# Last convolution in the gating tile, mixed blocks loaded a K tile at a time, conditioning sums by VectorE, attention's place kept free of the last weights

## The chip, the cores and the metric

The kernel runs on one core of a Trainium2 chip. A core has five engines that work through instruction lists of their own and meet at semaphores: TensorE (PE, with its weight loads as PEld), VectorE (DVE), ScalarE (ACT), GpSimd (POOL) and SyncE (SP), which here only issues loads. Transfers run on 16 DMA engines. The metric is the device time of one execution in microseconds (us), as a median over runs; a shorter time is better.

## The reference

One layer of a hybrid backbone over 2048 tokens of width 1024 (a grid of 32 rows by 64 columns), with 256 context tokens. Everything is float32.

```python
mod_l = jnp.split((jax.nn.silu(c) @ ada_w[l] + ada_b[l])[:, None, :], 6, axis=-1)
h = _modulate(_rmsnorm(x, norm1_g[l]), mod_l[0], mod_l[1])
z = h @ w_in[l]            # columns: q, k, v (512 each), gating u, v (256 each), conv a, gate (256 each)
kvc = hc @ w_in[l][:, ATT_W:3 * ATT_W]                       # keys, values of the context
att = _neighbourhood_attention(q, k, v, kc, vc, na_rpb[l], rows)   # 8 x 16 window, 8 heads
sg = _spatial_gating(u, v, ...)      # gelu(u) * (chunks of 128 tokens of norm(gelu(v)), mixed by w_s)
cv = _conformer_conv(a, gate, ...)   # 31-tap depthwise convolution, group norm, silu
y = jnp.concatenate([att, sg, cv], axis=-1) @ w_out
x = x + mod_l[2] * y
h2 = _modulate(_rmsnorm(x, norm2_g[l]), mod_l[3], mod_l[4])
x = x + mod_l[5] * _conv_ffn(h2, ffn_w_up[l], ffn_conv_w[l], ffn_conv_b[l], ffn_w_down[l])
return _rmsnorm(x, final_norm_g)
```

## The kernel before

The 2048 tokens are four blocks of 512 (`TB`), numbered 0 to 3. A float32 product is made of three matmuls on a high and a low part of each operand (suffixes `h` and `l`); the parts come from a copy on ACT (L228, L249) and a subtraction on DVE or POOL (L229, L252). All matmuls go through `mm` (L204), all loads through `load` (L195, queue of SP), most stores through `store` (L198, queue of POOL).

The program has these stages, by the profile's time. A setup to about 60 us makes block 0's input. **Stage 1**, to about 300 us, weaves several generators together: `stage1()` with the projections of blocks 0 and 1 (k, convolution, gating, v, q), the row statistics of the input (`stats`), `ada_rest` and the convolution of block 0 (`conv_range(0)`). **Attention**, to about 1010 us, is `attend()`: 128 units, each a band of rows, a pair of heads, a column block and one head of the pair. A unit has `scores` (matmuls into the bank `s`, one reduction on DVE that adds the bias and finds the maximum, L695, the exponential on ACT, L698), `turned` (transposes `tp`, copied to `pt` by ACT, L728, and DVE, L730) and, for each two units, `values`. Between these the generator `fill()` puts the projections of blocks 2 and 3 and the output projections, and from units 0, 45 and 80 on the convolutions of blocks 1, 2 and 3 run beside them, one step for each unit. After that come the end of the output projection, the feed-forward layer's upper half (to about 1925 us) and its lower half.

PE's instructions up to the end of attention are pinned to the order of the program. A scheduler orders the other engines by priority and by its own estimate of times: what is inside `hot` gets a high priority, `issue_after` forbids an instruction to stand ahead of another.

Names that the change touches:

- PSUM in stage 1: a ring `g` of five banks for the projections, one bank `m`, two banks `ad`. `m` takes the mean and scale banks of a convolution (`cvm`, `cvv`, `cvr`), the row norms' factors (`h1ms` to `h3ms`, made by `rstd`) and the gating's mixing (`sgp`, made by `gating_tail` and emptied by the DVE instruction `sgm`, L509).
- `conv_range(b)`: two accumulators `cv` (two channel tiles), begun by ACT (L569) and continued by 30 taps each on DVE (L575); then mean (L585), variance, scale (L610), silu (L613), split, and a store into `mixd`. The accumulators come from a ring `acc` of two, so each convolution waits until the one before has been stored.
- The gating tile (tag `gu`, one buffer): u and v of one block; it is free once the block's gating has been stored in `mixd`.
- `ada_rest`: the conditioning columns that are not needed at once. For each of 16 groups two 512 KB tiles `adaf` are loaded (a ring of three), scaled by silu(c) row by row on ACT (L965, eight instructions), and added up on POOL (L968, L969, L970: 1024, 512 and 256 elements).
- `mixd` holds the concatenated [att, sg, cv] of each block in memory; `load_mix(b)` brings all eight K tiles, high and low part (`mxh`, `mxl`), into the place of the blocks' h, for the output projection.
- Weights come through `load_w`: a staging tile, and rings of three for the high and the low part; every fourth weight takes a buffer of another pool, in the list `wxp`, as long as that list is not empty. The attention pool is opened over the place of that pool and of the stage's other ones.
- `h2xa`, `h3xa`: pieces of the input of blocks 2 and 3; `qq`, `kk`, `vt`, `vcx`, `bias_t`: what a unit of attention loads; `qs`, `ks`, `vs` are where q, k, v lie in memory.

Of the kernel before, what the change touches and what calls it, by code (L numbers as in the profile page):

```python
# [143 lines left out]
def tile_hybrid_block(ctx: ExitStack, tc: tile.TileContext, a, out):  # L144
# [157 lines left out]
    mbufs = 1  # L302

    def add_square(acc, x, n, name, eng, pool):
        if acc is None:
# [258 lines left out]
    def conv_range(b):  # L564

        hb = hcv[b]
        acc = [jp.tile([P, TB], F32, bufs=2, tag="acc", name=f"cv{b}{ct}") for ct in range(2)]
# [34 lines left out]
        nc.vector.reciprocal(col, col)  # L602
        yield
# [47 lines left out]
    qk, biases = {}, {}  # L651

    def scores(band, pr, cb, j, pool):

        if (band, pr, j) not in qk:
            head_tiles(band, pr, j, pool)
        qq, kk = qk[band, pr, j]
        r0, nr = ROWS[band]
        kr0, knr, kc0, knc = key_box(band, cb)
        n = knr * knc  # L660
        nch, rp = chunking(band, cb)
        ck = rp * knc
        rt, ct = RTYPE[band], CTYPE[cb]
        nm = f"{band}{pr}{cb}{j}"
        if (band, pr, ct, j) not in biases:
            bt = bias_tile(pool)
            load(bt[:, 512 - n:512], a[f"bias{rt}{ct}"][2 * pr + j])
            biases[band, pr, ct, j] = bt
        bt = biases[band, pr, ct, j]
        if cb == 0 and j == 0:  # L670
            heads[band, pr] = pair_tiles(band, pr, pool)
        vcx, hl, rs = heads[band, pr]
        if j == 0:
            vt = pool.tile([P, 4, P], F32, tag="vt", name=f"vt{band}{pr}{cb}", bufs=4)
            vsr = vs[0:SEQ].rearrange("(r c) f -> r c f", c=64)
            for i in range(nch):
                load(vt[0:ck, i, :],
                     vsr[kr0 + i * rp:kr0 + (i + 1) * rp, kc0:kc0 + knc, pr * P:(pr + 1) * P])
            steps[band, pr, cb] = vt, [], []
        if cb == 3 and (band, pr) != (NB - 1, 3):  # L680
            head_tiles(band + (pr == 3), (pr + 1) % 4, j, pool)
        s = pp.tile([P, 1024], F32, tag="s", name="s" + nm)
        qs_ = slice(cb * P, (cb + 1) * P)
        kv = kk[:, 0:1024].rearrange("p (r c) -> p r c", c=64)[
            :, kr0 - r0:kr0 - r0 + knr, kc0:kc0 + knc]
        so = s[:, 512 - n:512].rearrange("p (r c) -> p r c", c=knc)
        for i in range(2):
            mm(so, qq[:, i, qs_], kv, start=(i == 0), stop=(i == 1))
        for i in range(2):
            mm(s[:, 512:768], qq[:, i, qs_], kk[:, 1024:], start=(i == 0), stop=(i == 1))  # L690
        sb = pool.tile([P, 768], F32, tag="sb", name="sb" + nm, bufs=3)
        mx = cp.tile([P, 1], F32, tag="mx", name="mx" + nm, bufs=3)
        w = slice(512 - n, 768)

        x = nc.vector.tensor_tensor_reduce(out=sb[:, w], in0=s[:, w], in1=bt[:, w], scale=-1.0,  # L695
                                           scalar=3.0e38, op0=ALU.add, op1=ALU.min, accum_out=mx)
        dve_marks.append(x.ins)
        nc.scalar.activation(sb[:, w], sb[:, w], AF.Exp, bias=mx, scale=-1.0, accum_out=rs[:, cb, j:j + 1])  # L698
        steps[band, pr, cb][1].append(sb)
# [76 lines left out]
    def attend(pool, fill, sides):  # L776
# [62 lines left out]
    def load_mix(b, ks_):  # L839
# [3 lines left out]
        more_mix(b, ks_)  # L843

# [87 lines left out]
    jp = wpool_.__enter__()  # L932
# [21 lines left out]
    def ada_rest():  # L954


        for g0 in range(8, 24, 4):
            res = adpool.tile([P, 4, 256], F32, tag="adar", bufs=1, name=f"adar{g0}")
            for i in range(4):
# [8 lines left out]
                nc.gpsimd.tensor_tensor(t, t, t_, op=ALU.add)  # L968
                nc.gpsimd.tensor_tensor(t[:, 0:2, :], t[:, 0:2, :], t[:, 2:4, :], op=ALU.add)  # L969
                nc.gpsimd.tensor_tensor(res[:, i, :], t[:, 0, :], t[:, 1, :], op=ALU.add)  # L970
# [40 lines left out]
    def stage1():  # L1011
# [22 lines left out]
        rstd("h3", TB)  # L1034
        yield from proj_q((1,))
# [14 lines left out]
    def fill():  # L1050
# [602 lines left out]
```

## Time and profile before

| | |
|---|---|
| time of three runs | 2357.55, 2360.74, 2363.66 us; median 2360.74 |
| the profiled execution's own time | 2365.48 us |
| its span | 2363.7 us |
| PE busy | 2268.4 us, 96% of the span |
| DVE, ACT, POOL busy | 72%, 48%, 34% |
| mean granted clock of TensorE | 0.982 |
| HBM traffic | 471 MB, 199 GB/s over the span |

The profile is one execution, recorded by the hardware, and all durations below are its. A row of waits reads "engine tile line <- what released it: total us, times, longest us". A row of the timeline reads "start, duration, engine, line, operation, out<-in", with the idle time of the engine ahead of it and its releaser in brackets. A row of groups has the count, then the busy time and the mean in ns, then the idle time ahead. The granted clock is a share of full speed.

### The profile page before, as it was taken

The numbers are of one execution on the slowest core, as the hardware profiler recorded it, in microseconds if no ns is written. First come the engines' busy times: TensorE is split into PE (matmuls) and PEld (weight loads), VectorE is DVE, ScalarE is ACT, GpSimd is POOL, SyncE is SP. The second block draws the span as 40 slices with busy tenths as digits, with TensorE's granted clock in tenths as the row PEclk, the third lists the DMA queues.
The fourth block names the chain that finished last, engine by engine and source line by source line (L and its number), as shares of the span: only waits on it lengthen the run. The fifth ranks groups of instructions, "written<-read, shape, count | busy, mean of one in ns | idle before, by whom it ended". The sixth has DMA issues, their size and how long they took to land.

```text
span 2363.7 us, 34634 instructions
## 1 busy us (share of the span) xinstructions
PE 2268.4 (96%) x12474; PEld 1898.5 (80%) x12474; DVE 1710.7 (72%) x2552; ACT 1138.6 (48%) x2019; POOL 793.8 (34%) x844
## 2 busy tenths in 40 slices
PE   7999999999899899999999999999999999999998
PEld 5889777997788688878787788778788878888886
DVE  4787556556685694697888887788888777578565
ACT  4765643347455446564444443434333445454443
POOL 0255412111011132225566665455656432002000
PEclk8999999999999999999999999999999999999999
DMA  9675486557879679662444533745553368557653
GB/s 347 230 263 172 168 263 188 180 168 231 258 199 285 199 211 289 231 204 85 138 170 146 181 134 108 270 179 211 210 208 111 98 232 298 196 191 249 204 194 116
DMA packets 203868, 473.63 MB, mean 200 GB/s; under 512 B 21808, under 2 KB 70832, under 8 KB 202672
## 3 DMA queue, kind: packets, MB, share of 16 engines
q1 hardware_dynamic: 166160, 359.20, 47.5%
q0 software_dynamic: 31488, 105.93, 12.0%
q10 hardware_dynamic: 6048, 6.29, 0.8%
q8 instruction: 98, 1.61, 0.3%
q14 instruction: 74, 0.61, 0.1%
HBM read 352.06 MB, written 119.28 MB: 199 GB/s over the span
## 4 chain that ended last, share of the span: by engine, by line
PE 52%; DVE 15%; issue 13%; DMA 12%; ACT 4%; POOL 2%; SPq 1%; POOLq 0%; DVEq 0%; ACTq 0%
PE po L204 4%; PE p L1481 4%; PE pu L1481 4%; PE obank L204 3%; PE pk L204 3%; DMA adaf<-in_ada 3%; PE pv L1481 3%; PE s L204 2%; PE tp L210 2%; PE tp L204 2%; PE pq L204 2%; DMA wds<-in_w_down 2%; SPq L195 1%; DVE cv L575 1%; PE tg L204 1%
## 5 line engine op out<-in xcount | busy, mean ns | idle before, releaser
L575 DVE SCALAR_TENSOR_TENSOR cv<-hconv,cst,cv 128x512 f32<-128x512 f32 x240 | 215.6, 940 | 11.4 <-ACT cv L569 11.2
L1103 DVE TENSOR_TENSOR dw<-wd,dw 128x512 fp32r<-128x512 f32 x154 | 114.1, 749 | 103.3 <-ACT dw L1102 100.8
L1481 PE MATMUL pu<-ah,dw 128*128 128x512 f32 x792 | 181.7, 390 | 0.0
L698 ACT ACTIVATE sb<-sb,mx 128x544 f32<-128x544 f32 (+3 forms) x128 | 106.3, 830 | 154.8 <-DVE mx L695 148.8
L695 DVE CUSTOM_DVE_ANT_0 sb<-s,bias_t 128x544 f32<-128x544 f32 (+3 forms) x128 | 105.1, 821 | 101.7 <-PE s L204 78.3
L1481 PEld LDWEIGHTS pu<-ah,dw 128*128 128x128 f32 x792 | 148.7, 188 | 31.8 <-issue 1.0
L1102 ACT ACTIVATE dw<-wd 128x512 fp32r<-128x512 f32 x154 | 96.0, 628 | 159.7 <-PE pu L1481 58.3
L1481 PE MATMUL p<-ah,dw 128*128 128x512 f32 x528 | 122.5, 394 | 2.4 <-DVE u L1330 2.4
L1481 PE MATMUL pv<-ah,dw 128*128 128x512 f32 x528 | 120.3, 389 | 0.0
L1481 PEld LDWEIGHTS p<-ah,dw 128*128 128x128 f32 x528 | 100.2, 190 | 24.3 <-DVE u L1330 2.9
L204 PE MATMUL s<-kk,qq 128*128 128x256 f32 (+4 forms) x512 | 102.5, 323 | 16.3 <-DVE mx L695 10.2
L204 PEld LDWEIGHTS s<-kk,qq 128*128 128x128 f32 x512 | 89.5, 192 | 34.5 <-DVE mx L695 14.7
L1481 PEld LDWEIGHTS pv<-ah,dw 128*128 128x128 f32 x528 | 99.1, 188 | 20.6
L1367 ACT ACTIVATE c<-c 128x512 f32<-128x512 f32 x88 | 55.3, 630 | 124.9 <-DVE c L1365 124.6
L210 PE MATMUL tp<-cst,sb 128*128 128x128 f32 (+2 forms) x672 | 97.1, 275 | 13.0 <-DVE pt L730 9.0
L210 PEld LDWEIGHTS tp<-cst,sb 128*128 128x128 f32 (+2 forms) x672 | 79.9, 138 | 31.6 <-DVE pt L730 9.9
L1103 POOL TENSOR_TENSOR ah<-ra,ah 128x512 fp32r<-128x512 f32 x22 | 32.9, 1510 | 210.2 <-ACT ah L1102 208.8
L1102 ACT ACTIVATE ah<-ra 128x512 fp32r<-128x512 f32 x154 | 93.9, 617 | 10.6 <-DMA ra<-actd 10.5
L1103 DVE TENSOR_TENSOR ah<-ra,ah 128x512 fp32r<-128x512 f32 x132 | 92.2, 701 | 4.2 <-ACT ah L1102 4.2
L1365 DVE SCALAR_TENSOR_TENSOR cs<-gb,cst,cs 128x512 f32<-128x512 f32 x84 | 62.9, 749 | 21.9 <-ACT cs L1363 21.6
L728 ACT ACTIVATE pt<-tp 128x384 f32<-128x384 f32 (+2 forms) x128 | 61.2, 478 | 36.6 <-PE tp L210 36.0
L965 ACT ACTIVATE adaf<-adaf,silu_c 128x256 f32<-128x256 f32 x128 | 54.2, 497 | 50.5 <-DMA adaf<-in_ada 50.5
(1662 smaller groups left out, 7044.7 us busy)
## 6 DMA issues: line engine op xcount, KB each, us to landing
ra<-actd SPq DMA_DIRECT2D x70, 512.0 KB
wg<-in_w_up SPq DMA_DIRECT2D x44, 512.0 KB
wu<-in_w_up SPq DMA_DIRECT2D x44, 512.0 KB
actd<-tt POOLq DMA_DIRECT2D x88, 256.0 KB, 2.4
wd<-sd SPq DMA_DIRECT2D x40, 512.0 KB
actd<-c POOLq DMA_DIRECT2D x66, 256.0 KB, 2.4
adaf<-in_ada SPq DMA_DIRECT2D x32, 512.0 KB
qq<-qs SPq DMA_DIRECT2D x64, 256.0 KB
```

What stands on the lines that cost most here:

```text
L204: x = nc.tensor.matmul(*args, **kw)
L210: x = nc.tensor.transpose(*args)
L575: nc.vector.scalar_tensor_tensor(acc[ct], hb[:, ct, k:k + TB], cvw[:, ct, k:k + 1], acc[ct], op0=ALU.mult, op1=ALU.add)
L695: x = nc.vector.tensor_tensor_reduce(out=sb[:, w], in0=s[:, w], in1=bt[:, w], scale=-1.0, scalar=3.0e38, op0=ALU.add, op1=ALU.min, accum_o ...
L698: nc.scalar.activation(sb[:, w], sb[:, w], AF.Exp, bias=mx, scale=-1.0, accum_out=rs[:, cb, j:j + 1])
L728: nc.scalar.activation(dst, src, AF.Copy)
L965: nc.scalar.activation(t[:, k, :], t[:, k, :], AF.Copy, scale=silu_c[:, k0 + k, 0:1])
L1102: nc.scalar.activation(hl[:, 0, :], src, AF.Copy)
L1103: eng.tensor_tensor(hl[:, 1, :], src, hl[:, 0, :].bitcast(F32), op=ALU.subtract)
L1365: nc.vector.scalar_tensor_tensor(to, gb[:, i, o + d:o + d + TB], fcw[:, f, d:d + 1], ps, op0=ALU.mult, op1=ALU.add)
L1367: nc.scalar.activation(c, c, AF.Silu)
L1481: nc.tensor.matmul(ps[i], w[:, ww, sl], ah[:, aa, :], start=start and k_ == 0 and m == 0, stop=(k_ == NP - 1 and m == 2), skip_group_check ...
```

## The change

It has six parts. The number of instructions of each kind stays the same, except that 48 additions go from POOL to DVE.

1. The accumulators of the last convolution (b = 3), and one tile of squares of the output projection, are parts of the gating tile after the last gating (`rest`), not of the ring `acc`.
2. `rstd`, and `gating_tail` for blocks 0 and 1, take a bank of the ring `g` instead of `m`.
3. `conv_range` pauses one step more ahead of the rescaling.
4. The loads of the first ten units of attention are placed at normal priority instead of the high one.
5. `mix_steps(b)` places the loads of mixed blocks 0 and 1 one K tile at a time, each behind attention's latest bias or vt load, woven into the convolution and gating projections of block 3 (block 0) and into the output projection (block 1).
6. `ada_rest` adds on DVE, and the list `wxp` is emptied ahead of the q projection of block 1, so that stage 1's last weights take the common rings and attention's place comes free sooner.

```diff
+    def rest_tile():
+        if not rest:
+            rest.append(jp.tile([P, 4 * TB], F32, tag="gu", bufs=1, name="rest"))
+        return rest[0]
...
     def rstd(name, n):
-        ps = pp.tile([P, TB], F32, tag="m", bufs=mbufs, name=name + "ms")
+        ps = g_bank(name + "ms")
...
     def gating_tail(b):
...
-            ps = pp.tile([P, TB], F32, tag="m", bufs=mbufs, name=f"sgp{b}{ct}")
+            ps = g_bank(f"sgp{b}{ct}") if b < 2 else pp.tile([P, TB], F32, tag="m", bufs=mbufs, name=f"sgp{b}{ct}")
...
     def conv_range(b):
-        acc = [jp.tile([P, TB], F32, bufs=2, tag="acc", name=f"cv{b}{ct}") for ct in range(2)]
+        if b == NB - 1:
+            acc = [rest_tile()[:, (1 + ct) * TB:(2 + ct) * TB] for ct in range(2)]
+        else:
+            acc = [jp.tile([P, TB], F32, bufs=2, tag="acc", name=f"cv{b}{ct}") for ct in range(2)]
...
         nc.vector.reciprocal(col, col)
         yield
+        yield
...
-    def scores(band, pr, cb, j, pool):
+    def scores(band, pr, cb, j, pool, loads=None):
+        with (loads or hot)():
             ...   # the loads of qq, kk, bias, vcx, vt; att_load[0] keeps the latest bias or vt load
+        with hot():
             ...   # matmuls, reduction, exponential
...
-                with hot():
-                    scores(*units[u + 2], pool)
+                scores(*units[u + 2], pool, nullcontext if u < 8 else None)
...
+    def mix_steps(b):
+        load_mix(b, ())
+        for k in (4, 5, 6, 7, 0, 1, 2, 3):
+            with tc.issue_after(att_load[0]):
+                more_mix(b, (k,))
+            yield
...
-                nc.gpsimd.tensor_tensor(t, t, t_, op=ALU.add)
-                nc.gpsimd.tensor_tensor(t[:, 0:2, :], t[:, 0:2, :], t[:, 2:4, :], op=ALU.add)
-                nc.gpsimd.tensor_tensor(res[:, i, :], t[:, 0, :], t[:, 1, :], op=ALU.add)
+                nc.vector.tensor_tensor(t, t, t_, op=ALU.add)
+                nc.vector.tensor_tensor(t[:, 0:2, :], t[:, 0:2, :], t[:, 2:4, :], op=ALU.add)
+                nc.vector.tensor_tensor(res[:, i, :], t[:, 0, :], t[:, 1, :], op=ALU.add)
...
         rstd("h3", TB)
+        wxp.clear()
         yield from proj_q((1,))
...
-        yield from proj_conv(3, h["h3"])
-        yield from proj_gating(3, h["h3"])
+        yield from weave(chain(proj_conv(3, h["h3"]), proj_gating(3, h["h3"])), mix_steps(0), 4.0)
         yield from weave(proj_q((3,)), gating_tail(3), 8.0)
-        yield from out_proj((0, 1))
+        yield from weave(out_proj((0, 1)), mix_steps(1), 0.6)
```

Three places show how instructions move. The first is SP's queue at the start of attention: the last pieces of block 2's input (`h2xa`), pieces of block 3's (`h3xa`), weights (`wa21s`, `wk20s`), and the first unit's `qq` and `kk`. Before:

```order
L195 DMA h2xa_2869<-in_xT 128x512
L195 DMA h2xa_2875<-in_xT 128x512
L195 DMA h3xa_3080<-in_xT 128x512
L195 DMA wa21s<-in_w_f 128x1024
L195 DMA h3xa_3086<-in_xT 128x512
L195 DMA h3xa_3092<-in_xT 128x512
L195 DMA wk20s<-in_w_f 128x1024
L195 DMA h3xa_3098<-in_xT 128x512
L195 DMA qq_3162<-qs 64x1024 x2
L195 DMA kk_3165<-ks 128x768
L195 DMA kk_3165<-ks 128x256
```

In the changed kernel the same place reads:

```order
L195 DMA h2xa_2869<-in_xT 128x512
L195 DMA h2xa_2875<-in_xT 128x512
L195 DMA qq_3162<-qs 64x1024 x2
L195 DMA kk_3165<-ks 128x768
L195 DMA kk_3165<-ks 128x256
L195 DMA bias_t_3168<-in_bias 128x288
L195 DMA vcx_3175<-vs 128x2x128
L195 DMA vt_3179<-vs 96x1x128 x3
L195 DMA qq_3208<-qs 64x1024 x2
L195 DMA kk_3211<-ks 128x768
L195 DMA kk_3211<-ks 128x256
L195 DMA bias_t_3170<-in_bias 128x288
```

The first `qq` and `kk` stand right behind the last `h2xa`; the weights and all pieces of `h3xa` come after the first two units' loads of q and k.

The second is SP's queue in the middle of attention, ahead of the bias of a new pair of heads (the row `bias_t_3172` at the end); `mxh` and `mxl` are mixed block 0, `vt` and `vcx` pieces of v, the names ending in s staging tiles of weights. Before:

```order
L195 DMA wt3g_1s<-in_w_tok 128x1024
L195 DMA mxh_7544<-mixd 128x512
L195 DMA mxl_7545<-mixd 128x512
L195 DMA mxh_7544<-mixd 128x512
L195 DMA vt_6189<-vs 128x1x128 x4
L195 DMA vt_6259<-vs 120x1x128 x3
L195 DMA vcx_6374<-vs 128x2x128
L195 DMA mxl_7545<-mixd 128x512
L195 DMA mxh_7544<-mixd 128x512
L195 DMA mxl_7545<-mixd 128x512
L195 DMA wu30s<-in_w_f 128x1024
L195 DMA bias_t_3172<-in_bias 128x360
```

In the changed kernel:

```order
L195 DMA wt3g_1s<-in_w_tok 128x1024
L195 DMA vt_6195<-vs 128x1x128 x4
L195 DMA vt_6267<-vs 120x1x128 x3
L195 DMA vcx_6384<-vs 128x2x128
L195 DMA mxh_6021<-mixd 128x512
L195 DMA mxl_6022<-mixd 128x512
L195 DMA mxh_6021<-mixd 128x512
L195 DMA mxl_6022<-mixd 128x512
L195 DMA wu30s<-in_w_f 128x1024
L195 DMA bias_t_3172<-in_bias 128x360
```

Between the k loads of the pair before and this bias, 14 of the 16 loads of mixed block 0 stood before (two further ahead) and 8 stand now; the other 8 come behind the next two k loads.

The third is ACT in the last third of attention: `sb` are exponentials, `pt` copies of transposes, `att` and `cvsq` splits ahead of stores. Before, the start of the last convolution (`cv_7791<-hconv_5932`) stands among the ends of block 2's (`cv_5997`, `cv_5998`):

```order
L613 ACTIVATE cv_5997<-cv_5997,cst 128x512
L698 ACT_TABLE_LOAD
L698 ACTIVATE sb_7952,rs_7628<-sb_7952,mx_7953 128x616
L228 ACTIVATE cvsq_7835<-cv_5997 128x512
L760 ACTIVATE att_7627<-obank 128x8x32
L728 ACTIVATE pt_7996<-tp_7997 128x384
L569 ACTIVATE cv_7791<-hconv_5932,cst 128x512
L613 ACT_TABLE_LOAD
L613 ACTIVATE cv_5998<-cv_5998,cst 128x512
L698 ACT_TABLE_LOAD
L698 ACTIVATE sb_8037,rs_7628<-sb_8037,mx_8038 128x616
```

In the changed kernel both starts stand at an earlier unit, behind the splits of the last gating (`gu_5933`) and the q projection of block 3:

```order
L746 ACTIVATE pt_7483<-tp_7484 128x384
L716 ACTIVATE sb_7476,rs_7224<-sb_7476,mx_7477 128x768
L249 ACTIVATE wo02h<-wo02s 128x1024
L568 ACTIVATE q_7501<-pq_7426 128x512
L584 ACTIVATE rest<-hconv_5932,cst 128x512
L716 ACTIVATE sb_7524,rs_7224<-sb_7524,mx_7525 128x616
L584 ACTIVATE rest<-hconv_5932,cst 128x512
L778 ACTIVATE att_7223<-obank 128x8x32
L746 ACTIVATE pt_7568<-tp_7569 128x384
L716 ACTIVATE sb_7603,rs_7224<-sb_7603,mx_7604 128x616
```

The two starts moved from the end of block 2's convolution to the unit in which the last gating is stored.

More of the change, by code (lines that the diff above doesn't have):

```diff
@@ L302, in tile_hybrid_block @@
     mbufs = 1
+    jp_ = [None]
+    rest = []
+    def rest_tile():
+        if not rest:
+            rest.append(jp.tile([P, 4 * TB], F32, tag="gu", bufs=1, name="rest"))
+        return rest[0]
     def add_square(acc, x, n, name, eng, pool):
-        if acc is None:
+        if acc is None and pool is jp_[0]:
+            sq = rest_tile()[:, 0:TB]
+        elif acc is None:
             sq = pool.tile([P, 4 * TB], F32, tag="gu", bufs=1, name="sq" + name)[:, 0:TB]
@@ L649, in pair_tiles @@
         return vcx, hl, rs
-    qk, biases = {}, {}
-    def scores(band, pr, cb, j, pool):
[L655 to L699, printed above, removed]
@@ new lines, in tile_hybrid_block @@
+    qk, biases, att_load = {}, {}, [None]
+    def scores(band, pr, cb, j, pool, loads=None):
+        with (loads or hot)():
+            if (band, pr, j) not in qk:
+                head_tiles(band, pr, j, pool)
+            qq, kk = qk[band, pr, j]
+            r0, nr = ROWS[band]
+            kr0, knr, kc0, knc = key_box(band, cb)
+            n = knr * knc
+            nch, rp = chunking(band, cb)
+            ck = rp * knc
+            rt, ct = RTYPE[band], CTYPE[cb]
+            nm = f"{band}{pr}{cb}{j}"
+            if (band, pr, ct, j) not in biases:
+                bt = bias_tile(pool)
+                att_load[0] = load(bt[:, 512 - n:512], a[f"bias{rt}{ct}"][2 * pr + j])
+                biases[band, pr, ct, j] = bt
+            bt = biases[band, pr, ct, j]
+            if cb == 0 and j == 0:
+                heads[band, pr] = pair_tiles(band, pr, pool)
+            vcx, hl, rs = heads[band, pr]
+            if j == 0:
+                vt = pool.tile([P, 4, P], F32, tag="vt", name=f"vt{band}{pr}{cb}", bufs=4)
+                vsr = vs[0:SEQ].rearrange("(r c) f -> r c f", c=64)
+                for i in range(nch):
+                    att_load[0] = load(vt[0:ck, i, :],
+                         vsr[kr0 + i * rp:kr0 + (i + 1) * rp, kc0:kc0 + knc, pr * P:(pr + 1) * P])
+                steps[band, pr, cb] = vt, [], []
+            if cb == 3 and (band, pr) != (NB - 1, 3):
+                head_tiles(band + (pr == 3), (pr + 1) % 4, j, pool)
+        with hot():
+            s = pp.tile([P, 1024], F32, tag="s", name="s" + nm)
+            qs_ = slice(cb * P, (cb + 1) * P)
+            kv = kk[:, 0:1024].rearrange("p (r c) -> p r c", c=64)[
+                :, kr0 - r0:kr0 - r0 + knr, kc0:kc0 + knc]
+            so = s[:, 512 - n:512].rearrange("p (r c) -> p r c", c=knc)
+            for i in range(2):
+                mm(so, qq[:, i, qs_], kv, start=(i == 0), stop=(i == 1))
+            for i in range(2):
+                mm(s[:, 512:768], qq[:, i, qs_], kk[:, 1024:], start=(i == 0), stop=(i == 1))
+            sb = pool.tile([P, 768], F32, tag="sb", name="sb" + nm, bufs=3)
+            mx = cp.tile([P, 1], F32, tag="mx", name="mx" + nm, bufs=3)
+            w = slice(512 - n, 768)
+            x = nc.vector.tensor_tensor_reduce(out=sb[:, w], in0=s[:, w], in1=bt[:, w], scale=-1.0,
+                                               scalar=3.0e38, op0=ALU.add, op1=ALU.min, accum_out=mx)
+            dve_marks.append(x.ins)
+            nc.scalar.activation(sb[:, w], sb[:, w], AF.Exp, bias=mx, scale=-1.0, accum_out=rs[:, cb, j:j + 1])
+            steps[band, pr, cb][1].append(sb)
@@ L792, in attend @@
         for u in range(2):
-            with hot():
-                scores(*units[u], pool)
+            scores(*units[u], pool)
             other(2.0)
@@ L931, in tile_hybrid_block @@
     wpool_ = tc.tile_pool(name="proj", bufs=1, side="right")
-    jp = wpool_.__enter__()
+    jp = jp_[0] = wpool_.__enter__()
     b2 = [jp.tile([P, P], F32, name=f"b2_{i}") for i in range(2)]
```

1 line of the change is left out of this document (removed).

## The prediction

> **What bounds the kernel now.** I read the page's busy table first. PE is busy for nearly the whole span, so a change that adds and removes no PE instruction can only win time in which PE stands still or runs at a reduced clock.
>
> ```profile
> PE 2268.4 (96%) x12474; PEld 1898.5 (80%) x12474; DVE 1710.7 (72%) x2552; ACT 1138.6 (48%) x2019; POOL 793.8 (34%) x844
> ```
>
> The windows view gives the stages (first row: all of stage 1; second: attention) and 30 us stretches in which PE was not full. Columns: length, busy time of PE, weight loads, DVE, ACT, POOL, granted clock, DMA share, GB/s.
>
> ```profile
> 60.00:300.00 240.00, 228.80 (x1462) 200.89 (x1462) 165.71 (x215) 149.57 (x283) 105.91 (x90) 0.99 0.63 210
> 300.00:1010.00 710.00, 679.69 (x5007) 584.45 (x5005) 458.46 (x874) 367.84 (x668) 134.72 (x138) 0.98 0.74 224
> 210.00:240.00 30.00, 26.55 (x204) 25.94 (x204) 9.27 (x10) 13.95 (x35) 14.75 (x8) 0.94 0.53 171
> 240.00:270.00 30.00, 25.89 (x140) 21.26 (x139) 13.64 (x10) 20.24 (x40) 17.00 (x9) 0.94 0.53 176
> 300.00:330.00 30.00, 26.07 (x117) 21.26 (x115) 22.34 (x42) 13.08 (x20) 6.90 (x10) 1.00 0.87 294
> 330.00:360.00 30.00, 26.06 (x120) 21.48 (x120) 13.85 (x25) 15.04 (x24) 4.72 (x2) 0.89 0.72 201
> 630.00:660.00 30.00, 25.27 (x203) 23.90 (x204) 20.98 (x42) 12.49 (x28) 0.57 (x1) 0.83 0.73 212
> 780.00:810.00 30.00, 20.31 (x128) 16.44 (x128) 18.55 (x34) 14.24 (x24) 3.46 (x5) 0.85 0.64 183
> 810.00:840.00 30.00, 29.71 (x231) 25.02 (x230) 29.80 (x50) 13.24 (x29) 8.34 (x7) 0.98 0.82 220
> ```
>
> A stall costs twice here: the wait itself, and the stretch at a reduced clock behind it. I price the second as length times (1 minus clock): 30 x 0.06 = 1.8 us in 210:240 and in 240:270, 30 x 0.11 = 3.3 in 330:360, 30 x 0.17 = 5.1 in 630:660, 30 x 0.15 = 4.5 in 780:810, 30 x 0.02 = 0.6 in 810:840: 17.1 us. This is an upper price, since time that PE waits anyway loses nothing to the clock.
>
> The waits of PE, asked for by stage (60:300, 300:370, 600:650, 700:820), say who released each: total, times, longest; one fence for each stage.
>
> ```profile
> PE h2ms L204 <- DVE cv L585: 4.1, 1, 4.1
> PE tp L204 <- ACT v L420: 3.4, 2, 2.9
> PE sgp L204 <- DVE sgm L509: 2.3, 1, 2.3
> PE sgp L204 <- DVE cv L610: 0.8, 1, 0.8
> ```
>
> ```profile
> PE s L204 <- DMA kk<-ks: 5.6, 1, 5.6
> PE s L204 <- DVE mx L695: 1.8, 1, 1.8
> PE tp L210 <- DVE pt L730: 1.1, 1, 1.1
> ```
>
> ```profile
> PE s L204 <- DVE mx L695: 6.6, 1, 6.6
> ```
>
> ```profile
> PE tp L210 <- DVE pt L730: 6.8, 2, 4.9
> PE tp L210 <- ACT pt L728: 2.9, 1, 2.9
> ```
>
> They sum to 35.4 us. With the clock, at most 52.5 us is to be had in these places; what lies behind attention the change does not touch.
>
> **The change part by part.**
>
> *The m bank in stage 1.* h2ms, h3ms and the gating banks of blocks 0 and 1 leave the one-bank ring "m" and take turns in the five-bank ring "g". The three waits on a DVE instruction that empties that bank (4.1, 2.3, 0.8) have no other cause: h2ms waits for a subtraction of the convolution that it has nothing to do with. They sum to 7.2, with the clock of 240:270 9.0. The g ring lengthens by one tile in use, whose wait would be on an eviction by ACT; the nearest rows are the 3.4 of tp behind ACT's v. The additional yield before the rescale gives the reciprocal one more PE step of cover; it removes nothing that the trace shows as long. I take 7.5, ends 3.5 and 9.
>
> *The conditioning sums on DVE.* 16 groups of three additions (1024, 512, 256 elements) leave POOL for DVE.
>
> ```profile
> L968 POOL TENSOR_TENSOR adaf<-adaf,adaf x16: 2374/2412/3065, 94.9 to 266.0; 128x1024 f32<-128x1024 f32 x16
> L252 DVE TENSOR_TENSOR wtv_0l<-wtv_0s,wtv_0h 128x1024 fp32r<-128x1024 f32 x2 | 2.4, 1219 | 4.5 <-ACT wtv_0h L249 4.5
> L229 DVE TENSOR_TENSOR k<-pk,k 128x512 fp32r<-128x512 f32 x4 | 2.7, 671 | 0.0
> L229 DVE TENSOR_TENSOR k<-pk,k 128x256 fp32r<-128x256 f32 x4 | 1.7, 414 | 0.2 <-ACT k L228 0.2
> L575 DVE SCALAR_TENSOR_TENSOR cv<-hconv,cst,cv 128x512 f32<-128x512 f32 x64 | 68.6, 1126 | 2.1 <-ACT cv L569 2.0
> L575 DVE SCALAR_TENSOR_TENSOR cv<-hconv,cst,cv x64: 715/741/3176, 112.3 to 291.2; 128x512 f32<-128x512 f32 x64
> 177.71 6.49 DVE L575 SCALAR_TENSOR_TENSOR cv<-hconv,cst,cv 128x512 f32<-128x512 f32 x4
> 177.73 2.40 POOL L968 TENSOR_TENSOR adaf<-adaf,adaf 128x1024 f32<-128x1024 f32 x1 [9.76 <-ACT adaf L965]
> POOL adaf L968 <- ACT adaf L965: 89.4, 13, 25.7
> ACT adaf L965 <- DMA adaf<-in_ada: 50.5, 22, 7.4
> ```
>
> By DVE rows of the same lengths a group costs 1.219 + 0.671 + 0.414 = 2.30 us, 36.9 for 16. Against that stands what POOL's additions do to DVE: convolution taps take 741 ns as a median but 1126 as a mean, up to 3176, and the slow ones lie beside an L968 as at 177.71, where four take 6.49 us for some 3.0. 64 x (1126 - 741) = 24.6 us come back on the taps alone, and the same happens to some weight splits. DVE's 165.71 us of 240 therefore stays about the same, with 74 us free. A group gets through about 2.5 us sooner, so its buffers return sooner to the loads; ACT, which stood in front of a late load before it could empty v (rows of 210:240: 3.4 of wait, 1.8 of clock), is helped a little, but the load itself paces that. I take 2 of 5.2; the ends are -4 and 5.2, since DVE now stands where POOL stood and waited 89.4 us for ACT.
>
> *Attention's place and first loads.* In SP's order the first qq and kk now follow the last piece of h2 directly; four loads of h3 and three of weights that stood ahead go behind them.
>
> ```profile
> 308.04 1.78 SPq L195 DMA_DIRECT2D h2xa<-in_xT  x2
> 322.12 1.16 SPq L195 DMA_DIRECT2D qq<-qs  x2
> ```
>
> qq was issued 322.12 - 309.82 = 12.3 us after the last h2 piece, kk right behind it, and PE waited 5.6 us for kk. If the new order lets them go even half of that sooner, the wait is gone; its clock (3.3) goes with it. For that the memory of the weights' second pool must be free, which the cleared list gives: the last four weights no longer sit in it. What is late next is h3's input, behind a dozen more issues of about 1 us, and with it DVE, which does those modulations ahead of score reductions; the 1.8 and 1.1 us of this stage's rows are of that kind and may grow. The last weights also have three buffers for each half where every fourth had a fourth one. Of 5.6 + 1.8 + 1.1 + 3.3 = 11.8 I take 8, ends -2 and 11.8.
>
> *Mixed blocks a K tile at a time.* 14 loads of mixed block 0 stood between the second kk and the bias that the next pair of heads needs; 8 stand there now.
>
> ```profile
> 613.81 8.64 SPq L195 DMA_DIRECT2D vt<-vs  x7
> 625.83 0.85 SPq L195 DMA_DIRECT2D bias_t<-in_bias  x2
> 633.87 0.80 DVE L695 CUSTOM_DVE_ANT_0 sb<-s,bias_t 128x616 f32<-128x616 f32 x1 [9.19 <-DMA bias_t<-in_bias]
> ```
>
> SP is never idle for long in front of this bias: the seven vt pieces alone take 8.64 us to issue, 1.23 each. At that price six loads fewer bring the bias some 7 us forward, and it also finds six 256 KB transfers fewer ahead of it in a window with DMA share 0.73. DVE's 9.19 us shrink to 2 or 3, of which PE, one unit ahead, feels none or one. The displaced eight follow at the next pair, where the same row of loads passes without a stall. 6.6 + 5.1 = 11.7; I take 10, ends 3 and 11.7. For block 1 SP's order does not change: nothing.
>
> *Last convolution in the gating tile.*
>
> ```profile
> 784.68 0.81 ACT L569 ACTIVATE cv<-hconv,cst 128x512 f32<-128x512 f32 x1 [8.79 <-DMA mixd<-cv]
> 799.40 0.81 ACT L569 ACTIVATE cv<-hconv,cst 128x512 f32<-128x512 f32 x1 [3.51 <-DMA mixd<-cv]
> 728.11 0.53 POOL L198 DMA_DIRECT2D mixd<-gu  x1 [2.00 <-DVE gu L229]
> DMA to landing us min/median/max: 6.2/6.8/7.4
> 732.31 0.81 ACT L698 ACTIVATE sb<-sb,mx 128x616 f32<-128x616 f32 x1
> ```
>
> ACT stood 8.79 and 3.51 us until block 2's convolution had been stored, with the evictions of attention queued behind it: that is PE's 6.8 + 2.9 = 9.7 and the clock of 4.5 + 0.6. With its own place this wait is gone. The new one is for the gating tile: its second store, issued at 728.11, lands about 734.3 to 735.5, and the two new activations stand in ACT's order right around the exponential that ran at 732.31. ACT may thus stand 2 to 3 us there; PE has a unit of work in hand, and I charge 2. The 30 taps now start 50 us sooner, two for each unit, in a stretch where DVE had slack, instead of in the stretch where it was 29.80 of 30 busy. 14.8 - 2 leaves 12.8; I take 11.5, ends 4 and 14.8.
>
> *Sum.* 7.5 + 2 + 8 + 10 + 11.5 = 39 us off the profiled execution, whose own time is 2365.48: 2326.5. The median of the three runs shown, 2360.74, is 4.7 lower. I cannot see whether the runs that were faster had shorter stalls of this kind; I let 3 us of the gain go for it, so 36 off the median: 2325.
>
> The Trainium skill (TensorE: Matmul & The Clock Gate, Part 1, "What's actually happening") says that the throttled state is the default and that one busy window of about 3.4 us lifts it, at half rate until then. By that rule each of the five drops would cost about 1.7 us, 8.5 in place of 17.1, and the forecast would be some 6 to 7 us less gain, an estimate of 2331. The rows decide against it: 5.1 us in 630:660 and 4.5 in 780:810 are more than one such window.
>
> **The rivals.**
>
> *Half of it comes back elsewhere.* Each stall removed lets PE run into the next late thing: h3's loads in 330:360, a later bias, the gating store, evictions when DVE's slack is used. For it speaks that DVE in 810:840 has no slack and DMA is at 0.87 in 300:330; against it that most of the waits named have a cause in order, not in rate. Half of 39 gives 2360.7 - 19 = 2342.
>
> *Everything goes.* All 52.5 us: 2308. Against it: the loads of the conditioning weights and the gating store remain.
>
> *Slower: DVE stands in line for ACT's scaled conditioning tiles.* POOL's 89.4 us of waiting would fall on DVE, with weight splits and evictions queued behind. 165.7 + 36.9 - 24.6 + 89.4 = 267 us against a stage of 240: 27 us over on rate alone. With the other 37 us gained the kernel is still faster; it turns slower if more than 44 us of the 89.4 reach PE (half of them), since 37 - 44 = -7. At 50 us the time is 2374. For it: DVE executes in order, and single waits of 25.7 us exist. Against it: those waits are POOL's idle time between groups, and DVE's order is laid with other work between them, so an addition need not be at the head while its tile is still far off.
>
> The Trainium skill (same page, "Architectural detail") calls DVE's queue strictly first in, first out, which is what this rival needs; no run here shows yet how much reaches PE.
>
> *It does not do what it says.* kk, the bias and the taps arrive no sooner because the transfers, not the places in the queue, are late (DMA share 0.73 to 0.87 in those windows); only the m bank's 7.5 remain at most, within a stage that waits for weights anyway: 2354 to 2361.
>
> **How the numbers follow.** About 0.3% (7 us) is what a measurement of this kernel can tell from no change. The forecast case has 0.58, 2325, its own range 2317 to 2334; half back 0.22 (2342); everything 0.07 (2308); no effect 0.07; slower by the DVE queue 0.06. The first three are faster, and half of the fourth: 0.89; same 0.05; slower 0.06. The range 2307 to 2347 takes in the first three cases, 0.87 together, less their tails.
>
> **What the changed profile would show.** If right: among PE's waits no h2ms behind cv, no kk near 326, none above 2 us at 600:650 and 700:820; the clock at 0.95 or more in the stretches that answer to 330, 630 and 780; the first qq right behind h2xa on SP; taps with a mean near 750 ns in stage 1. What would make it wrong: new PE waits behind DVE for weights or evictions between 100 and 300, with DVE waiting for ACT's adaf; a PE wait behind h3's modulation after 340; ACT standing more than 4 us at the gating store.

## The result and the profile after

The changed kernel took 2343.11 us as a median of four runs (2336.43 to 2346.47), the kernel before 2361.61 on the same chip: a ratio of 0.992, 95% interval 0.9894 to 0.9946. On another chip, with more runs, it was 0.9926 (0.9908 to 0.9944). That is 18 us saved: inside the range of 2307 to 2347, half of the 36 that were forecast, and what the rival "half of it comes back elsewhere" had said (2342).

The page of the changed kernel, first its span and the busy table:

```profile
span 2341.3 us, 34626 instructions
...
PE 2262.6 (97%) x12474; PEld 1892.8 (81%) x12474; DVE 1699.1 (73%) x2600; ACT 1137.3 (49%) x2019; POOL 713.9 (30%) x796
```

POOL has lost 80 us of work and DVE, with 48 more instructions, has lost 12. The windows of stage 1 and attention (length, then busy time of PE, weight loads, DVE, ACT, POOL, then clock, DMA share, GB/s):

```profile
60.00:300.00 240.00, 239.61 (x1531) 210.78 (x1530) 172.83 (x285) 155.08 (x293) 25.32 (x48) 1.00 0.67 227
300.00:1010.00 710.00, 682.78 (x5020) 585.28 (x5019) 465.14 (x880) 373.59 (x677) 134.86 (x136) 0.99 0.75 226
```

Stage 1 is full: 239.61 of 240 us at full clock, where it was 228.80 at 0.99. Attention is hardly fuller than before (682.78, then 679.69). PE's waits, for the stretches that answer to those of the prediction (60:300, 300:345, 640:675, 755:820):

```profile
PE b2p L204 <- DVE b L972: 0.4, 1, 0.4
```

```profile
PE s L204 <- DVE mx L713: 7.1, 2, 5.4
PE tp L210 <- ACT pt L746: 0.9, 1, 0.9
PE tp L210 <- DVE pt L748: 0.4, 1, 0.4
```

```profile
PE tp L210 <- DVE pt L748: 4.3, 1, 4.3
```

```profile
PE s L204 <- DVE mx L713: 1.8, 1, 1.8
PE tp L210 <- ACT pt L746: 1.2, 1, 1.2
PE tp L210 <- DVE pt L748: 0.5, 1, 0.5
```

Every wait named in stage 1 is gone. The wait for kk at attention's start has become one for a score reduction, of the same size; the wait for the bias has become one of 4.3 us some 50 us later; of the waits of the last convolution, 9.7 us, 3.5 are left.

PE's order is pinned up to the end of attention, so the same matmul group can be found in each trace, and the difference of its start in the two shows where time was won. The table gives this lead over the profiled execution of the kernel before, in us, for the changed kernel and for those of the experiments. At the end of stage 1, kernels with the same code up to there differ by 4 us (14.8 to 18.5), but they differ as much already at 63 us (-0.6 to 3.2); from there each of them gains 15.3 or 15.4. So the change of the lead from row to row says more than its height. Each column is a single execution: that of the kernel before took 2365.48 us, 4 more than its median, and that of last_conv_in_ring 2346.67, 7 less than its median.

| group (its start in the kernel before) | changed | sums_on_pool | rows_in_m_bank | start_as_before | mix_whole | mix_spread | last_conv_in_ring | no_pause_last_conv | before_sums_on_dve |
|---|---|---|---|---|---|---|---|---|---|
| first matmul with weight wg00 (63.2) | -0.6 | 2.9 | 1.0 | 1.9 | 3.2 | 2.8 | 2.9 | 1.6 | 2.5 |
| last gating bank of stage 1 (292.6) | 14.8 | 5.7 | 12.3 | 17.2 | 18.5 | 18.1 | 18.3 | 16.9 | 14.5 |
| scores of the 1st unit (331.7) | 20.6 | 11.5 | 18.1 | 18.6 | 24.3 | 23.9 | 24.1 | 22.8 | 15.3 |
| 6th unit (357.0) | 13.5 | 4.1 | 10.1 | 15.9 | 16.5 | 16.5 | 16.8 | 16.0 | 12.2 |
| 54th unit (614.7) | 14.5 | 4.7 | 12.1 | 16.3 | 18.7 | 19.4 | 16.9 | 16.8 | 11.0 |
| 58th unit (640.6) | 23.7 | 13.9 | 21.3 | 25.5 | 21.5 | 28.6 | 26.2 | 26.1 | 13.9 |
| 72nd unit (701.8) | 16.7 | 7.0 | 12.4 | 15.3 | 20.5 | 21.7 | 20.6 | 18.3 | 14.7 |
| 89th unit (780.5) | 16.3 | 5.5 | 13.0 | 15.8 | 18.8 | 18.5 | 20.6 | 18.6 | 15.4 |
| 118th unit (911.5) | 25.1 | 16.7 | 21.6 | 23.9 | 30.6 | 30.2 | 20.2 | 26.8 | 14.8 |
| 128th unit (960.7) | 18.9 | 8.6 | 15.7 | 16.7 | 23.0 | 23.4 | 13.5 | 25.0 | 14.8 |
| lower half's first group (1987.4) | 24.1 | 12.0 | 20.2 | 17.4 | 26.0 | 22.3 | 18.6 | 31.7 | 18.4 |

The column of the changed kernel tells where: 15.4 us in stage 1 (-0.6 to 14.8); nothing at attention's start, where 5.8 are won up to the first scores and 7.1 lost behind them (14.8, 20.6, 13.5); 2.2 around the mixed block, where 9.2 are won at the bias and 7.0 lost behind it (14.5, 23.7, 16.7); 8.8 at the last convolution (16.3 to 25.1); and a loss of 6.2 at attention's end that no term of the forecast had (25.1 to 18.9). The last row lies behind 1000 us of code that is the same in all; what is won or lost there (from -1.1 to +6.7) differs from execution to execution.

### The profile page after: what moved, and what is told of

Read it like the earlier page. It is cut to its first block, busy times and chain, and to the rows that moved or that the text cites. A ratio compares the mean times of both kernels' runs of the same rounds, so it can differ in the third digit from the quotient of the medians.

```text
span 2341.3 us, 34626 instructions
## 1 busy us (share of the span) xinstructions
PE 2262.6 (97%) x12474; PEld 1892.8 (81%) x12474; DVE 1699.1 (73%) x2600; ACT 1137.3 (49%) x2019; POOL 713.9 (30%) x796
## 4 chain that ended last, share of the span: by engine, by line
PE 33%; issue 9%; DVE 5%; DMA 3%; ACT 0%; POOL 0%; SPq 0%; POOLq 0%; DVEq 0%; ACTq 0%
PE p L1506 4%; PE pu L1506 4%; PE pv L1506 3%; DMA wds<-in_w_down 2%; PE u_9y L1335 1%; PE g_9y L1335 1%; PE u_8y L1335 1%; PE g_8y L1335 1%; PE u_7y L1335 1%; PE g_7y L1335 1%; PE u_6y L1335 1%; PE g_10y L1335 1%; PE g_5y L1335 1%; PE g_4y L1335 1%; PE u_4y L1335 0%
## 5 line engine op out<-in xcount | busy, mean ns | idle before, releaser
L1506 PEld LDWEIGHTS pu<-ah,dw 128*128 128x128 f32 x792 | 148.7, 188 | 31.7 <-issue 1.0
L590 DVE SCALAR_TENSOR_TENSOR cv<-hconv,cst,cv 128x512 f32<-128x512 f32 x180 | 135.2, 791 | 2.5 <-ACT cv L584 2.4
L1506 PEld LDWEIGHTS pv<-ah,dw 128*128 128x128 f32 x528 | 99.1, 188 | 20.5
L204 PEld LDWEIGHTS s<-kk,qq 128*128 128x128 f32 x512 | 88.8, 191 | 30.8 <-DVE mx L713 17.2
L1127 ACT ACTIVATE ah<-ra 128x512 fp32r<-128x512 f32 x154 | 93.8, 617 | 12.2 <-DMA ra<-actd 10.9
L1390 DVE SCALAR_TENSOR_TENSOR cs<-gb,cst,cs 128x512 f32<-128x512 f32 x84 | 62.9, 749 | 20.5 <-ACT cs L1388 20.2
L198 POOL DMA_DIRECT2D ks<-k x60 | 33.0, 554 | 142.0 <-ACT k L228 117.8
```

The costliest lines, as they stand in the source:

```text
L204: x = nc.tensor.matmul(*args, **kw)
L590: nc.vector.scalar_tensor_tensor(acc[ct], hb[:, ct, k:k + TB], cvw[:, ct, k:k + 1], acc[ct], op0=ALU.mult, op1=ALU.add)
L1127: nc.scalar.activation(hl[:, 0, :], src, AF.Copy)
L1390: nc.vector.scalar_tensor_tensor(to, gb[:, i, o + d:o + d + TB], fcw[:, f, d:d + 1], ps, op0=ALU.mult, op1=ALU.add)
L1506: nc.tensor.matmul(ps[i], w[:, ww, sl], ah[:, aa, :], start=start and k_ == 0 and m == 0, stop=(k_ == NP - 1 and m == 2), skip_group_check ...
```

## The experiments

Each kernel has a ratio to the kernel before on its own chip, with its 95% interval. The changed kernel's 0.992 and 0.9926 are what they compare with; 0.001 is 2.4 us.

**Parts undone.** *The sums on POOL again:*

```diff
-                nc.vector.tensor_tensor(t, t, t_, op=ALU.add)
+                nc.gpsimd.tensor_tensor(t, t, t_, op=ALU.add)
 ...
```

> The changed kernel with the three additions of each conditioning group on POOL again. Theory (the sums and the m bank each remove their own wait): the v stall of 3.4 us and its clock of 1.8 come back, convolution taps in stage 1 are slow again (mean near 1.1 us instead of 0.75): the lead over the kernel before at the end of stage 1 falls from 14.8 to about 10, and the time rises by 4 to 6 us (ratio to before near 0.994, after 0.992). Rival (the sums are worth nothing by themselves, the bank is all): lead of 13 to 15, ratio 0.991 to 0.993.

Ratio 0.9974 (0.996 to 0.9987): 12 us lost, twice what the theory said, and two thirds of the whole gain. Taps of the convolution in stage 1 (60:300), first in this kernel, then in the changed one: count, busy us, mean ns.

```profile
L590 DVE SCALAR_TENSOR_TENSOR cv<-hconv,cst,cv 128x512 f32<-128x512 f32 x64 | 68.6, 1127 | 3.2 <-ACT cv L584 3.0
```

```profile
L590 DVE SCALAR_TENSOR_TENSOR cv<-hconv,cst,cv 128x512 f32<-128x512 f32 x64 | 44.9, 743 | 2.5 <-ACT cv L584 2.4
```

The 24 us came back as expected. What they are worth is seen in the stretch 120 to 150, again first here, then in the changed kernel, and in PE's longest wait of stage 1 here:

```profile
120.00:150.00 30.00, 24.08 (x152) 20.79 (x150) 30.00 (x42) 20.32 (x41) 16.87 (x20) 0.89 0.73 241
```

```profile
120.00:150.00 30.00, 30.00 (x200) 26.36 (x199) 28.68 (x51) 24.87 (x52) 10.19 (x19) 1.00 0.85 299
```

```profile
PE pk L204 <- DVE sgm L520: 5.2, 1, 5.2
```

With the sums on POOL, DVE is busy for all 30 us with 42 instructions and PE waits 5.2 us for it, although the gating no longer sits in the bank m: the wait moved from `sgp` to `pk`, the next user of the same five banks. With them on DVE it does 51 instructions in less time. From 63 us to the end of stage 1 this kernel gains 2.8 us where the changed one gains 15.4; between the matmuls that started at 137.7 and 147.1 in the kernel before, its lead falls by 5.5 while the changed kernel's rises by 2.6, which is 8 of the 12.6 us. The wait of 3.4 us behind ACT's v, which the theory expected back, is 0.9 here.

*The row factors and gatings in the bank m again* (the two `g_bank` calls of the diff replaced):

> The changed kernel with the row factors and the gating of blocks 0 and 1 in the single bank m again. Theory: the waits of h2ms and sgp come back (7.2 us and 1.8 of clock), the lead at the end of stage 1 falls from 14.8 to 6 or 8, the time rises by 7 to 9 us (ratio 0.995 to 0.996). Rival (with DVE faster in stage 1 the bank is emptied soon enough): lead of 12 or more, less than 3 us.

Ratio 0.9938 (0.9917 to 0.9959), 3 to 4 us, between the two; the intervals overlap with the changed kernel's, so that the time alone does not settle it. In the trace stage 1 gains 11.3 us instead of 15.4. PE's wait for `h2ms` is back, with 2.7 us, that for `sgm` is not:

```profile
PE h2ms L204 <- DVE cv L600: 2.7, 1, 2.7
PE sgp L204 <- DVE cv L626: 0.8, 1, 0.8
```

*Attention's start as before* (the list not emptied, first loads at high priority):

> The changed kernel without the emptied list ahead of the last weights and with attention's first loads at high priority again. Theory (the start of attention wants the first units' loads, block 3's input and the next weights at the same time, and any order makes one of them late): the 5.6 us wait for kk comes back and the 5.4 us wait behind block 3's modulation goes, within 2 us of the changed kernel (ratio 0.991 to 0.993). Rival (the prediction's term): 8 us are lost (ratio 0.9955).

In the changed kernel the loads of the first two units keep the high priority as well; the normal one holds for the third to the tenth unit, eight in all.

Ratio 0.9927 (0.9902 to 0.9951): no difference that can be measured. The theory holds. PE waits for kk again, in place of the reduction:

```profile
PE s L204 <- DMA kk<-ks: 7.1, 2, 4.3
```

*Mixed blocks as a whole again* (`mix_steps` not woven in):

> The changed kernel with mixed blocks 0 and 1 loaded as a whole again, as before the change. Theory: the 6.6 us wait for the bias near 612 and its clock of some 5 come back, the wait for wq31 near 662 goes (4.3 and 3.4): 2 to 5 us more, 2345 to 2348. Rival (the prediction's term): the bias stall comes back and nothing goes, 10 us more, 2353.

Ratio 0.9895 (0.9875 to 0.9915): nothing lost, so both missed the time. The waits stand where the theory had them. Here DVE waits for the bias and PE 3.6 us for the reduction behind it (6.6 in the kernel before), and ACT's wait for the weight wq31 is 5.2 us; in the changed kernel the same weight keeps ACT 8.7 us:

```profile
612.35 0.80 DVE L713 CUSTOM_DVE_ANT_0 sb<-s,bias_t 128x616 f32<-128x616 f32 x1 [6.31 <-DMA bias_t<-in_bias]
...
PE s L204 <- DVE mx L713: 4.3, 4, 3.6
...
ACT wq31h L249 <- DMA wq31s<-in_w_f: 5.2, 1, 5.2
```

```profile
663.30 1.06 ACT L249 ACTIVATE wq31h<-wq31s 128x1024 fp32r<-128x1024 f32 x1 [8.71 <-DMA wq31s<-in_w_f]
```

Exponentials and copies stand behind that copy on ACT, a DVE copy of transposes stands behind one of them, and PE waits 4.3 us for it from 662 on. The lead from the 54th to the 72nd unit grows by 1.8 us with the whole blocks and by 2.2 with the steps; in the kernel before with the sums alone, whose blocks are whole too, it grows by 3.7. The steps win more at the bias (9.2 up to the 58th unit, 2.8 with whole blocks) and lose it again by the 72nd.

*The last convolution in the ring of two again* (and with it the tile of squares):

> The changed kernel with the last convolution in the ring of two accumulators again, so that it waits for block 2's stores. Theory: ACT's waits of 8.8 and 3.5 us and PE's 9.7 with about 4 of clock come back near 770 to 800: the lead that is won there (16.3 to 25.1) is gone, 8 to 12 us more (ratio 0.9955 to 0.997). Rival (the last convolution now ends elsewhere and the loss at 905 to 935 is due to it): that loss of 6 goes too and only 3 to 5 us are lost.

Ratio 0.9962 (0.9945 to 0.998), 9 us lost, at the place that the theory named (the lead stays at 20 where the changed kernel's rises by 8.8), but not by its mechanism. ACT's wait for the stores is 1.1 us in the profiled execution, which was the fastest of ten. The taps begin only then, at 770, and fill DVE:

```profile
780.00:795.00 15.00, 11.13 (x46) 8.69 (x47) 15.00 (x27) 5.94 (x11) 2.83 (x3) 0.77 0.52 157
795.00:810.00 15.00, 14.84 (x119) 12.77 (x118) 15.00 (x27) 6.37 (x14) 1.85 (x2) 1.00 0.73 183
```

Taps stand in rows of up to five in front of reductions and copies there; in the changed kernel they begin at 729.3, two to a unit. The lead is 26.9 us at the 91st unit, behind the place of the old wait, and 19.6 at the 99th; the changed kernel has 24.4 at both. In this execution the late start is the cost, and not ACT's standing. How the two share the loss in the kernel before, where ACT stood 8.79 us, is not shown.

**Where the gain of attention's start went.** The changed kernel's DVE:

```profile
314.09 0.75 DVE L349 SCALAR_TENSOR_TENSOR h3t<-h3xa,a,h3r 128x512 f32<-128x512 f32 x1 [6.63 <-DMA h3xa<-in_xT]
...
318.50 0.72 DVE L713 CUSTOM_DVE_ANT_0 sb<-s,bias_t 128x544 f32<-128x544 f32 x1
```

The first score matmuls started at 311.1. Their reduction stood behind two modulations of block 3, whose input had been put behind the first units' loads. So I put the modulation behind the reduction:

```diff
-    run_all(x_block(3))
...
+        while not dve_marks:
+            yield
+        g = x_block(3)
+        ...  with tc.issue_after(dve_marks[-1]): next(g)      # a piece at a time, in the woven convolution projection
```

> The changed kernel, with the modulation of block 3's input placed one piece at a time behind attention's latest score reduction; SP's order of loads stays nearly the same. Theory (DVE in line): in the changed kernel the first score reduction stood behind two modulations that waited 6.6 us for their input, PE waited 5.4 us for it and ran 6.8 us at half clock. With the reduction ahead both go: PE's wait near 313 under 1.5 us, clock 1.00 there, 5 to 8 us less, 2335 to 2338. Rival (the loads of the first units are late anyway): a wait of 3 us or more for kk or the bias takes its place, 2341 to 2345.

The theory fell. The ratio is 0.9905 (0.9883 to 0.9926), not measurably better than the changed kernel, and the wait grew; the rival had its time and the size of its wait, but the wait is behind a weight, not behind kk or the bias:

```profile
PE s L204 <- DVE mx L713: 9.4, 1, 9.4
```

```profile
319.81 1.06 ACT L249 ACTIVATE wa20h<-wa20s 128x1024 fp32r<-128x1024 f32 x1 [12.83 <-DMA wa20s<-in_w_f]
```

The first reduction ran at 311.7, but ACT stood 12.83 us for the next weight, wa20, which SP issues behind the v pieces of the first units; behind it stood the part of the modulation for which DVE then waited. So I put the v pieces a unit later and the modulation behind the third reduction (and left out the pause of the last convolution, below):

```diff
+                if len(dve_marks) < 6:
+                    owed_vt.append(vt_loads)       # issued after the next unit of the second head
+                else:
+                    vt_loads()
...
+        while len(dve_marks) < 3:
+            yield 0
```

> The changed kernel without the pause in the last convolution, and with attention's start put in the order of need: the v pieces of the first units are loaded one unit later, and the modulation of block 3's input starts behind the third score reduction. Theory (the stall near 313 is a question of order: input of block 3 and weight wa20 stand behind v pieces that are needed 30 us later): PE's wait there falls from 5.2 to under 2.5 us, no more than one half-clock window, 3 to 7 us less than without the pause alone (its ratio was 0.9876): ratio 0.9845 to 0.9865. Rival (rate: too much has to be moved between 295 and 320): a wait of 4 us or more stays, 0.987 to 0.989.

Ratio 0.9882 (0.9862 to 0.9902): the rival by its time, though no single wait reaches its 4 us. Two groups of waits, 6.8 us together where the changed kernel's reductions had 7.1, took the place of the one, the second behind the weight after that:

```profile
PE s L204 <- DVE mx L720: 3.6, 2, 3.3
PE tp L210 <- ACT pt L756: 3.2, 1, 3.2
```

```profile
326.42 1.06 ACT L249 ACTIVATE wk20h<-wk20s 128x1024 fp32r<-128x1024 f32 x1 [5.68 <-DMA wk20s<-in_w_f]
```

In four orders of the same loads (before, changed, and these two) something that was needed came late: kk, h3's input, wa20, or wa20 and wk20.

**The mixed block, spread further.** The loads of a K tile after each 7.0 us of PE work:

```diff
-        yield from weave(chain(proj_conv(3, h["h3"]), proj_gating(3, h["h3"])), mix_steps(0), 4.0)
-        yield from weave(proj_q((3,)), gating_tail(3), 8.0)
+        yield from weave(chain(proj_conv(3, h["h3"]), proj_gating(3, h["h3"]),
+                               weave(proj_q((3,)), gating_tail(3), 8.0)), mix_steps(0), 7.0)
```

> The changed kernel, with a step of mixed block 0's loads after every 7.0 us of PE work in place of 4.0, up into the q projection of block 3. Theory (places in the queue): the weight wq31, 8.7 us in landing and 4.3 us of PE near 662, is late because displaced mix loads stand ahead of it; spread out they stand there less, the wait falls under 2 us and its clock goes: 4 to 7 us less, 2336 to 2339. Rival (rate): what has to be moved until then is nearly the same, so that waits of the same sum appear between 600 and 700: 2341 to 2346.

Ratio 0.9896 (0.9874 to 0.9919), and the rival again: wq31 keeps ACT for 5.1 us instead of 8.7, yet PE's wait there is 5.4, since now the bias was late too, and then the weight behind it:

```profile
659.08 1.06 ACT L249 ACTIVATE wq31h<-wq31s 128x1024 fp32r<-128x1024 f32 x1 [5.14 <-DMA wq31s<-in_w_f]
```

**The end of attention.** In the changed kernel an exponential whose maximum was ready at 921.2 ran at 927.07. ACT did this first:

```profile
922.48 0.63 ACT L320 ACTIVATE sqn<-x 128x512 f32<-128x512 f32 x1 [2.63 <-DMA mixd<-cvsq]
923.02 0.61 ACT L897 ACTIVATE ssum<-x 128x512 f32<-128x512 f32 x1
923.65 1.28 ACT L629 ACT_TABLE_LOAD   x1
924.95 0.81 ACT L629 ACTIVATE rest<-rest,cst 128x512 f32<-128x512 f32 x1
925.78 1.28 ACT L716 ACT_TABLE_LOAD   x1
927.07 0.83 ACT L716 ACTIVATE sb<-sb,mx 128x640 f32<-128x640 f32 x1
```

The second silu of the last convolution, with its two table loads, falls into the unit in which ACT also squares the output projection's tiles for the norm. PE's waits there (905:935) are short:

```profile
PE s L204 <- DVE mx L713: 1.2, 1, 1.2
PE n20ms L204 <- DVE rest L626: 1.2, 1, 1.2
```

About half of the 6.2 us is the clock, which is at 0.50 from 920.9 to 927.7. That drop begins after the second of these waits, for the rescaling of the same convolution, and ahead of the late exponential, so the exponential is not the whole cause. The additional pause puts the silu there. Without it in the last convolution alone:

```diff
         yield
-        yield
+        if b < NB - 1:
+            yield
```

> The changed kernel without the additional pause ahead of the rescaling in the last convolution alone. Theory: the pause moves the second silu of that convolution into the unit in which ACT also squares the output projection's tiles, so that exponentials come late and PE loses 6 to 7 us of its lead between 905 and 935; without it this loss is under 2 us: 2337 to 2339. Rival (it is the place to which 20 us of lead have moved that end, not the pause): the loss stays, 2341 to 2345.

Ratio 0.9876 (0.9857 to 0.9895), the lowest of all, 2336.62 us where the kernel before took 2365.96. From the 118th to the 128th unit the lead falls by 1.8 us instead of 6.2. The clock drops there still, but for 3.4 us instead of 6.8. The rival falls: in each of the seven columns with the pause the lead drops there by 5.9 to 8.1 us, also where it was only 16.7 before, and in the two without it by 1.8 and nothing. The theory holds that the pause is the cause. How much time it costs is less certain. By the ratios the gain is some 11 us, but the three other kernels of the same session lie at 0.9895 to 0.9905, only 5 to 7 us above this one. In the trace 4.4 us are won at this place; the execution is 9.6 us shorter, and the rest stands in places where the code is the same and is not explained.

**Three more runs.** The changed kernel once more, the sums alone in the kernel before, and whole blocks in the kernel with the start in order:

> The changed kernel itself, for a ratio on the same chip as the next three. All theories: ratio to before 0.990 to 0.9945, 2340 to 2350.

> The kernel before with one part of the change: the additions of the conditioning groups on DVE. Theory (POOL's additions slow DVE down where DVE is full, 120 to 150 and 180 to 210, and PE waits there for the gating and for v): taps at a mean of 0.75 us, waits for sgm and v gone, a lead of 6 to 10 us at the end of stage 1, ratio 0.995 to 0.997. Rival (the sums help only together with the new banks, which stop PE from standing at the bank m): lead under 3 us, ratio above 0.998.

> The same with mixed blocks 0 and 1 loaded as a whole, as before the change. Theory (loading them K tile by K tile moves one wait of 4 to 7 us from the bias near 612 to the weight wq31 near 660, and is worth nothing): within 2.5 us of the kernel with the steps. Rival (the steps win): 4 us or more slower.

The first gave 0.9926, as above. The sums alone gave 0.9946 (0.9928 to 0.9964): 13 of the 18 us. In stage 1 they gain 12.0 us (2.5 to 14.5) of the 15.4 that all parts together gain there. PE's waits of stage 1 fall from 10.6 us in four places to these:

```profile
PE h2ms L204 <- DVE cv L585: 2.1, 1, 2.1
PE sgp L204 <- DVE cv L610: 0.8, 1, 0.8
```

The last gave 0.9879 (0.9859 to 0.9898) against 0.9882 with the steps: the order of the mixed block's loads is worth nothing that can be measured.

The version to keep is the changed kernel without the pause in its last convolution. Its interval lies below that of the changed kernel's second measurement; neither reordering of the start improved on it.

## Why the prediction was right, and where it was wrong

The direction, the range and the places were right; the forecast was twice the effect. That the time fell inside the range is in part luck: the sums gained ten us more than their term, which makes up for about half of the 18 that the two terms on SP's queue did not bring. By its terms, with the leads of the changed kernel and what the runs showed:

- *The m bank* (7.5) and *the sums* (2). Together 9.5 predicted, 15.4 in the trace, but the shares were the wrong way round. In stage 1 the sums alone gain 12.0; the bank adds about 4 to them (11.3 without it, 15.4 with it), and without the sums the other parts gain 2.8. The step that failed is that the waits on the bank "have no other cause": with the sums alone the wait for `sgm` is gone and that of `h2ms` halved, and with the new banks and POOL's sums the wait for `sgm` comes back on another tile, 5.2 us long where it was 2.3. It was the slowed DVE's. The prediction had read DVE's load as 165.71 of 240, "with 74 us free", but in the stretch of the kernel before in which PE waited for `sgm` DVE had no free time:

```profile
120.00:150.00 30.00, 27.54 (x189) 24.20 (x188) 30.00 (x41) 21.28 (x44) 17.57 (x19) 1.00 0.76 258
```

  The 24.6 us that the taps were to give back were nearly right (68.6 to 44.9); they were not counted as time on the path.
- *Attention's start* (8). Nothing. The first scores did come 5.8 us sooner. The prediction saw what would be late next, "h3's input", and charged 3.8 us for it; it cost the whole, 5.4 us and a half clock behind it, like the wait that went. In none of the four orders was every load in time between 295 and 330; whether another order could do it is not shown. The weights wa20 and wk20, which the prediction moved without a price, are in the same line.
- *The mixed block* (10). 2.2, no more than kernels with whole blocks gain there (1.8 and 3.7). At the bias the term was nearly right, 9.2 us. The sentence that failed is that the eight displaced loads pass "without a stall": they keep ACT 3.5 us longer at wq31 and PE 4.3, with the clock behind that, 7.0 of lead. And the price was that of one execution: PE's wait for the bias is 6.6 us in the profile of the kernel before, but 3.6 in `mix_whole` and in `before_sums_on_dve`.
- The rival that described these two is "half of it comes back elsewhere" (0.22), by its time and by h3's loads. The one that said kk and the bias would arrive no sooner (0.07) is wrong in that: both did, and the next load was late instead.
- *The last convolution* (11.5). 8.8; the sign, place and near size were right. The new wait for the gating's store was 2.2 us on ACT (2 to 3 predicted) and PE did not feel it:

```profile
717.75 0.82 ACT L584 ACTIVATE rest<-hconv,cst 128x512 f32<-128x512 f32 x1 [2.20 <-DMA mixd<-gu]
```

  The mechanism was half right: the prediction gave all of the price to ACT's wait, and named the taps in a stretch where DVE was full without a price. In the run that undoes the part it is the taps, starting late and crowding DVE, that cost.
- *The pause* was costed at a benefit too small to see. It cost 4 to 6 us of lead at attention's end, a loss that no term had.
- *The slower rival*, DVE standing in line for the scaled tiles, did not come. POOL's 89.4 us of waiting became 24.9 on DVE, in pieces of at most 6.0, none of which PE noticed:

```profile
DVE adaf L993 <- ACT adaf L990: 24.9, 10, 6.0
```

The clock, priced from the rows at 17.1 us, went as far as the waits went: stage 1 and 780 to 810 run at 1.00, while there are new drops: 316.8 to 323.6, 664.9 to 671.7 and 920.9 to 927.7 run at 0.50, each worth up to 3.4 us.

One sum is off: the chance of a faster kernel, given as 0.89, is 0.905 by the cases listed (0.58, 0.22, 0.07 and half of 0.07).

## What to carry to other kernels

A wait that is named after a buffer may be the slowness of the engine that empties it: look at that engine's busy share in the 30 us around the wait, not in the stage, and at whether its instructions take their usual time there. A wait for a load in a stretch in which the queue hardly rests was only moved by other orders of the loads here; price it as moved until a run shows otherwise, and ask which load is needed next. After a change has won time early, look at what the engines do together at the new places late in the program: a step that is one unit later can put two table loads in front of an exponential.

## What the runs showed of the hardware

A drop of the clock can follow shorter waits than I had in mind. The changed kernel's stretch 915 to 930 has no wait of PE above 1.2 us, and yet a granted clock of 0.77:

```profile
915.00:930.00 15.00, 13.13 (x64) 9.91 (x62) 5.25 (x11) 11.46 (x18) 5.93 (x7) 0.77 0.80 271
```

The Trainium skill (TensorE: Matmul & The Clock Gate, "HAM oscillation — how this bites in real kernels") gives as a rule that PE should have no idle gap above about 3.4 us; this row shows a drop without one. The Trainium skill (same page, "A second HAM failure mode: psum-queue depth-cycling") describes a kernel in which frequent short idling between groups of matmuls does it. Whether that is the cause here, and how much of it is needed, no run here tells.
